# A list scheduler's table of operation times, latencies and landing times, refitted to recorded durations

## The chip, the cores and the metric

The kernel runs on one core of one Trainium2 chip. The metric is device time in microseconds. TensorE (PE) does matmuls and its weight loads (PEld in the profile), VectorE is DVE, ScalarE is ACT, GpSimd is POOL, and SyncE (SP) issues the DMAs.

## The reference, cut to what matters

A decoder trunk of two layers for 1024 tokens of width 1024. Layer 0 mixes tokens by a causal Conformer convolution, layer 1 by sliding-window attention (16 query heads, 4 key heads, window 128). After each mixer come a layer norm, an MLP with squared ReLU (width 4096), a second norm and a gated embedding of width 256:

```python
for i in range(DEPTH):
    if i < N_A_LAYERS:
        y = conformer_conv(x, conv_w_in[i], ...)          # x @ w_in, gate, depthwise conv, LN, SiLU, @ w_out
    else:
        kk, vv = shared_banded_kv(x, kv_w_k, kv_w_v, cos, sin)
        y = swa_sink_attention(x, attn_w_q[j], attn_sinks[j], attn_w_o[j], kk, vv, cos, sin)
    x = layer_norm(DEEPNORM_ALPHA * x + y, mix_ln_g[i], mix_ln_b[i])
    x = layer_norm(DEEPNORM_ALPHA * x + sq_relu_mlp(x, mlp_w_up[i], mlp_w_down[i]), mlp_ln_g[i], mlp_ln_b[i])
    x = x + (p[i] @ ple_w_proj[i]) * jax.nn.sigmoid(x @ ple_w_gate[i])
```

## The kernel before

**Arithmetic.** Every operand of a matmul is held as two parts: a high part (ScalarE copies it to the type fp32r) and a low part (VectorE subtracts the high part from the value); `split` (L719) makes both, and `mm3` (L723) spends three matmuls on a product, high by high, high by low and low by high. In the profile's names h and l at the end of a tile's name are these parts: wh and wl of a weight, xh and xl of x. Large products are cut by two-by-two schemes with seven products instead of eight, so sums of weight blocks and of token blocks (forms) are made on VectorE ahead of them; some forms are stored to DRAM (`gate_t`, `gate_low_t`, `hid`) and loaded again.

**Stages**, in the order of the program, with their time in the profile before: the convolution and its output product (`conv`, L883, `conv_seven` L940, `mix_out` L1333) up to about 250 us; the first MLP (`mlp` L1486, `down_seven` L1641), up to about 1015; the first gated embedding (`ple`, L1765), up to about 1080; attention (`attention`, L1915), up to about 1390, its output product and norm up to about 1430; the second MLP up to about 2010; the second embedding. Tokens go in tiles of 128 rows and columns in halves of 512, so that a matmul is mostly 128x512; a unit of weights is a tile of 128x1024 in raw (as loaded), wh and wl.

**Attention's values.** `values` (L2146) takes four heads of probabilities in z, transposes them on PE (ps<-ident,z), splits the result on ScalarE and VectorE into two tiles A, lets GpSimd mask both by affine_select into two more tiles A (`own_keys`, L2173), and multiplies all four by the values in v, z or bo.

**What sets the order.** No order is written out. The program is recorded first: `Recorder` keeps every operation with its inputs, its tiles and a priority, which is the place in the program plus an offset. `schedule` (L337) is a list scheduler: it always takes the engine that is free first, and on it the operation of the lowest priority that is ready by its own clock. Its clock has four parts: `cost` (L306) gives the length of an operation, `delay` in `schedule` the time from the end of one operation to the start of another that needs it, the block on SP the time at which a DMA lands, and `both` holds VectorE and GpSimd apart where it deems them to share a port. Tiles get slots from pools (SLOTS, L52: five slots for t, nine for A, six PSUM banks for ps), and a slot goes to the next tile in line when its last user has ended by that clock. Operations marked "either" (adds of the layer norm in `layer_norm`, L812ff, and of the embedding, L1801) go to VectorE or to GpSimd, whichever the clock has free first. `issue` (L478) then emits the operations in the order found, so all instructions carry its line, L488 (L499 after the change). On the chip each engine runs its instructions in this order and waits on semaphores, so the clock's numbers act through the order, the slots and the engine of the "either" adds, and through nothing else.

The functions that the diff touches, and what calls them:

Of the kernel before, what the change touches and what calls it, by code (L numbers as in the profile page):

```python
# [13 lines left out]
ALU = mybir.AluOpType  # L14
# [6 lines left out]
HT = 512  # L21
# [57 lines left out]
MIX_WORK = (2, 4), (0,)  # L79
UP_NEXT = 4, 6, 0, 2  # L80
DOWN_WORK = {0: [("w_q", range(4))], 1: [("w_q", range(4, 8))], 2: [("w_o", range(4))], 3: [("w_o", range(4, 8))]}, {}
Q_AHEAD = 2
PAIRS_AHEAD = (0,), (0, 2)
GRAIN = 64
# [131 lines left out]
class Recorder:  # L216
# [90 lines left out]
    def cost(self, o, outs, allv):  # L307
        e, n = o.eng, o.name
        f = outs[0].n if outs and isinstance(outs[0], View) else 1024
        if e == "tensor":  # L310
            if n == "transpose":
                return 113.5
            return max(109.0, f * 0.4427 + 5.5 * (f < HT))
        if e == "sync":
            return 380.0
        if e == "scalar":
            t = 60.0 + f * 0.85
            if n == "activation":
                t += sum(c for k, c in (("bias", 90.0), ("scale", 130.0), ("accum_out", 110.0)) if isinstance(o.kw.get(k), View))
            return t  # L320
        if e == "gpsimd":
            if n == "tensor_tensor":
                return 460.0 if o.kw["op"] == ALU.pow else 120.0 + 2.3 * f
            return 160.0 + 1.17 * f
        psum = any(v.buf.space == "PSUM" for v in allv)
        if n == "tensor_scalar" and not psum:
            return 100.0 + f * 0.69
        if n == "bn_stats":
            return 69.0 + 1.042 * allv[-1].n
        if n == "reduce_max":  # L330
            return 70.0 + allv[-1].n * 1.042
        if n == "reciprocal":
            return 60.0 + 6.3 * f
        t = 120.0 if isinstance(o.kw.get("scalar"), View) else 70.0
        return t + f * 1.042

    def schedule(self):  # L337
        import heapq
# [25 lines left out]
        dma = 0.0  # L364
        lanes = [0.0] * 8
        order = []
        lat = 200.0
        same = dict(vector=127.0, scalar=93.0, gpsimd=100.0)

        def delay(o, x):  # L370
            a, b = o.eng, x.eng
            if a in ("alloc", "sync") or b == "alloc":
                return 0.0
            if a == b:
                return same.get(a, 0.0)
            return 200.0 if a == "tensor" else 400.0 if b == "tensor" else 240.0

        def enable(o):
            if o.eng == "alloc":
# [44 lines left out]
        while True:  # L424
            best = None
            for e in engs:
                while rdy[e] and rdy[e][0][2].end:
                    heapq.heappop(rdy[e])
                while fut[e] and fut[e][0][3].end:
                    heapq.heappop(fut[e])  # L430
                if rdy[e]:
                    t = free[e]
                elif fut[e]:
                    t = max(free[e], fut[e][0][0])
                else:
                    continue
                if best is None or t < best[0]:
                    best = (t, e)
            if best is None:
                break  # L440
            t, e = best
            while fut[e] and fut[e][0][0] <= t:
                r, p, i, o = heapq.heappop(fut[e])
                if not o.end:
                    heapq.heappush(rdy[e], (p, i, o))
            p, i, o = heapq.heappop(rdy[e])
            if WAIT and fut[e] and e != "tensor":
                r, p2, i2, o2 = fut[e][0]
                if not o2.end and r <= t + WAIT and p2 < p - 300:
                    heapq.heappush(rdy[e], (p, i, o))  # L450
                    heapq.heappop(fut[e])
                    t, o = r, o2
            if o.eng == "either":
                o.eng = e
                o.dur = self.cost(o, o.outv, o.allv)
            d = o.dur
            if e == "scalar" and o.name == "activation":
                k = TABLE.get(o.args[2].name if len(o.args) > 2 else "", 0)
                if k and k != table:
                    table = k  # L460
                    d += 1283.0
            if both(o):
                d += max(0.0, held["gpsimd" if e == "vector" else "vector"] - 50.0 - t)
                held[e] = t + d
            free[e] = t + d
            if e == "sync":
                lane = max(t, lanes.pop(0))
                free[e] = lane + d
                dma = max(dma, lane + 1400.0) + max(v.transfer() for v in o.allv)
                lanes.append(max(dma, lane + 4000.0))  # L470
                finish(o, lanes[-1])
            else:
                finish(o, t + d)
# [47 lines left out]
class Emit:  # L521
# [964 lines left out]
    def mlp(self, i):  # L1486
# [90 lines left out]
        for n, cs in enumerate(DOWN):  # L1577
            self.down_seven(i, cs, n == 0, n == len(DOWN) - 1, list(range(NT)) if n == RES else [])
            nc.slack = WORK_SLACK
            for what, ks in DOWN_WORK[i].get(n, ()):  # L1580
                for k in ks:
# [748 lines left out]
```

## Time and profile before

| | us |
|---|---|
| three runs of the kernel | 2099.75, 2100.91, 2102.42 |
| their median | 2100.91 |
| the profiled execution | 2101.52 |
| its span (first to last instruction) | 2099.8 |
| PE busy, DVE busy, ACT busy, POOL busy | 2082.9, 1700.9, 1207.1, 295.1 |

A row of the timeline has the start, the length, the engine, the operation and its tiles (result <- sources, without slot numbers), and, in brackets, the idle time of the engine ahead of it with what ended that. A run of equal instructions stands in one row with its count (x4), its length from the first start to the last end. Matmuls overlap in their records.

### The profile page before, as it was taken

The numbers are of one execution on the slowest core, as the hardware profiler recorded it, in microseconds if no ns is written. First come the engines' busy times: TensorE is split into PE (matmuls) and PEld (weight loads), VectorE is DVE, ScalarE is ACT, GpSimd is POOL, SyncE is SP. The second block draws the span as 40 slices with busy tenths as digits, with TensorE's granted clock in tenths as the row PEclk, the third lists the DMA queues.
The fourth block names the chain that finished last, engine by engine and source line by source line (L and its number), as shares of the span: only waits on it lengthen the run. The fifth ranks groups of instructions, "written<-read, shape, count | busy, mean of one in ns | idle before, by whom it ended". The sixth has DMA issues, their size and how long they took to land.

```text
span 2099.8 us, 29286 instructions
## 1 busy us (share of the span) xinstructions
PE 2082.9 (99%) x9784; PEld 1729.3 (82%) x9784; DVE 1700.9 (81%) x2631; ACT 1207.1 (57%) x2224; POOL 295.1 (14%) x513
## 2 busy tenths in 40 slices
PE   9999999999999999999999999999999999999999
PEld 7888888888888888888888888877888888888877
DVE  8999789987876889987963587989787778888688
ACT  6777654766666644345742488656666563333374
POOL 0533114000000000002220265520000000000040
PEclk9999999999999999999999999999999999999999
DMA  6669864878776879875566877587878785575635
GB/s 226 192 202 296 294 197 143 298 265 273 269 270 216 307 257 319 279 262 215 171 211 192 319 227 238 188 298 249 269 259 275 254 285 200 181 247 171 233 126 191
DMA packets 239063, 502.01 MB, mean 239 GB/s; under 512 B 24128, under 2 KB 62784, under 8 KB 238912
## 3 DMA queue, kind: packets, MB, share of 16 engines
q1 hardware_dynamic: 238912, 500.14, 71.2%
q8 instruction: 77, 1.26, 0.2%
q14 instruction: 74, 0.61, 0.1%
HBM read 337.26 MB, written 160.17 MB: 237 GB/s over the span
## 4 chain that ended last, share of the span: by engine, by line
PE 88%; DVE 5%; DMA 3%; ACT 2%; issue 1%; POOL 1%; SPq 0%; DVEq 0%; ACTq 0%; POOLq 0%
PE ps L488 67%; PE tr L488 21%; DVE z L488 1%; DMA wh<-gate_t 1%; ACT z L488 1%; DVE g L488 1%; POOL sm L488 1%; DMA raw<-in_w_up_dram 1%; DVE wl L488 1%; DVE B L488 1%; DVE xl L488 0%; DVE t L488 0%; DVE v L488 0%; DVE sm L488 0%; DVE X L488 0%
## 5 line engine op out<-in xcount | busy, mean ns | idle before, releaser
L488 PE MATMUL ps<-xh,xl 128*128 128x512 f32 x618 | 240.5, 389 | 0.0
L488 PE MATMUL ps<-xl,xh 128*128 128x512 f32 x618 | 240.5, 389 | 0.0
L488 PE MATMUL ps<-xh 128*128 128x512 f32 x618 | 240.5, 389 | 0.0
L488 POOL TENSOR_SCALAR sm<-sm 128x1 f32<-128x1 f32 x72 | 26.8, 374 | 1362.9 <-DVE E L488 1200.1
L488 PE MATMUL ps<-xl,wh 128*128 128x512 f32 x536 | 210.3, 393 | 0.4 <-DVE xl L488 0.4
L488 PE MATMUL ps<-xh,wh 128*128 128x512 f32 x536 | 209.4, 393 | 0.8 <-DVE xl L488 0.5
L488 PE MATMUL ps<-xh,wl 128*128 128x512 f32 x536 | 210.0, 392 | 0.0
L488 ACT CAST wh<-raw 128x1024 fp32r<-128x1024 f32 (+2 forms) x130 | 115.5, 890 | 77.5 <-PE ps L488 47.9
L488 PE MATMUL ps<-wh,xh 128*128 128x512 f32 (+1 forms) x352 | 138.5, 395 | 3.2 <-DMA wh<-gate_t 1.2
L488 PE MATMUL ps<-wh,xl 128*128 128x512 f32 (+1 forms) x352 | 138.6, 394 | 0.1
L488 PE MATMUL ps<-wl,xh 128*128 128x512 f32 (+1 forms) x352 | 138.6, 394 | 0.0
L488 ACT CAST xh<-wh 128x1024 fp32r<-128x1024 f32 x76 | 79.7, 1049 | 99.7 <-PE ps L488 53.0
L488 PEld LDWEIGHTS ps<-xh 128*128 128x128 f32 x618 | 116.0, 188 | 24.2
L488 PEld LDWEIGHTS ps<-xh,xl 128*128 128x128 f32 x618 | 116.0, 188 | 24.1
L488 ACT CAST wh<-g 128x512 fp32r<-128x512 f32 x136 | 81.2, 618 | 94.9 <-PE ps L488 52.6
L488 PEld LDWEIGHTS ps<-xl,xh 128*128 128x128 f32 x618 | 116.1, 188 | 23.9
L488 DVE TENSOR_TENSOR wl<-raw,wh 128x1024 fp32r<-128x1024 f32 (+2 forms) x96 | 93.2, 972 | 37.0 <-ACT wh L488 35.8
L488 DVE TENSOR_TENSOR wl<-g,wh 128x512 fp32r<-128x512 f32 x136 | 90.9, 690 | 38.5 <-ACT wh L488 38.4
L488 PEld LDWEIGHTS ps<-xh,wh 128*128 128x128 f32 x536 | 100.9, 188 | 21.9 <-DVE xl L488 0.7
L488 PEld LDWEIGHTS ps<-xl,wh 128*128 128x128 f32 x536 | 101.0, 188 | 21.1 <-DVE xl L488 1.1
L488 PEld LDWEIGHTS ps<-xh,wl 128*128 128x128 f32 x536 | 100.9, 188 | 20.7
L488 ACT ACTIVATE t<-t 128x512 f32<-128x512 f32 x144 | 90.8, 632 | 34.9 <-DVE t L488 33.3
(406 smaller groups left out, 5644.6 us busy)
## 6 DMA issues: line engine op xcount, KB each, us to landing
wh<-hid SPq DMA_DIRECT2D x78, 512.0 KB, 4.6
raw<-in_w_up_dram SPq DMA_DIRECT2D x68, 512.0 KB, 4.3
wl<-in_w_down_dram SPq DMA_DIRECT2D x58, 512.0 KB, 5.3
hid<-zz SPq DMA_DIRECT2D x96, 256.0 KB, 4.8
hid<-t SPq DMA_DIRECT2D x64, 256.0 KB, 4.7
z<-in_w_dw_dram SPq DMA_DIRECT2D x56, 288.0 KB, 4.1
raw<-hid SPq DMA_DIRECT2D x30, 512.0 KB, 4.7
xh<-in_w_gate_dram SPq DMA_DIRECT2D x32, 256.0 KB, 5.6
```

The costliest lines, as they stand in the source:

```text
L488: getattr(getattr(nc, o.eng), o.name)(*a, **k)
```

## The change

Three constants are new, and `cost`, `delay` and the landing time take other numbers. The operations, their priorities, the pools and the rest of the scheduler are the same. Of the numbers: a scalar operation of 512 columns goes from 495 to 475 ns with a PSUM operand and to 522 without; a GpSimd add of 512 from 1298 to 1610, an affine_select of 512 from 759 to 623, a GpSimd operation of one column from 161 to 272, its power from 460 to 545; between engines, PE to others goes from 200 to 297 (358 to GpSimd), others to PE from 400 to between 360 and 403; a DMA lands 700 later where the transfers before it set its time.

```diff
+TO_PE = 300.0
+MARGIN = 100.0
+LANDING = 700.0
...
         if e == "tensor":
-            if n == "transpose":
-                return 113.5
-            return max(109.0, f * 0.4427 + 5.5 * (f < HT))
+            return 109.0 if n == "transpose" else max(109.0, (f + 32) / 2.4)
...
         if e == "scalar":
-            t = 60.0 + f * 0.85
+            t = 40.0 + 0.85 * f if psum else 95.0 + 0.833 * f
             if n == "activation":
-                t += sum(c for k, c in (("bias", 90.0), ("scale", 130.0), ("accum_out", 110.0)) if isinstance(o.kw.get(k), View))
+                t += sum(c for k, c in (("bias", 90.0), ("scale", 95.0), ("accum_out", 96.0)) if isinstance(o.kw.get(k), View))
...
         if e == "gpsimd":
             if n == "tensor_tensor":
-                return 460.0 if o.kw["op"] == ALU.pow else 120.0 + 2.3 * f
-            return 160.0 + 1.17 * f
+                return 545.0 if f == 1 else 100.0 + 2.95 * f
+            if n == "memset":
+                return 85.0 + 0.82 * f
+            if n == "affine_select":
+                return 60.0 + 1.1 * f
+            if n == "tensor_copy":
+                return 120.0 + f
+            return 272.0 if f <= 8 else 170.0 + 1.3 * f
+        if n == "tensor_copy" and not psum:
+            return 65.0 + 0.52 * f
...
-        t = 120.0 if isinstance(o.kw.get("scalar"), View) else 70.0
-        return t + f * 1.042
+        if n == "bn_aggr":
+            return 118.0
+        return 66.0 + f * 1.042
...
-        same = dict(vector=127.0, scalar=93.0, gpsimd=100.0)
+        same = dict(vector=130.0, scalar=137.0, gpsimd=100.0)
+        seen = dict(tensor=163.0, vector=95.0, scalar=103.0, gpsimd=60.0)
...
-            return 200.0 if a == "tensor" else 400.0 if b == "tensor" else 240.0
+            return seen[a] + (TO_PE if b == "tensor" else MARGIN + (95.0 if b == "gpsimd" else 34.0))
...
-                lanes.append(max(dma, lane + 4000.0))
+                lanes.append(max(dma + LANDING, lane + 4000.0))
```

What the new clock does to the order: PE has the same 9784 matmuls, of which 2902 stand at another place, by 2.1 places on average and 76 at most; the first difference is at 20.8 us of the profile before, and in 400 to 1000 and 1500 to 2000 us PE's order hardly differs. On DVE 2036 of 2597 operations move, on ACT 1099 of 2058, on POOL 364 of 511, and of SP's 1500 DMAs 793. Ten "either" adds go from DVE to POOL and eight from POOL to DVE. Slots are dealt out anew. Three places follow, each with the rows of the order, the kernel before first.

PE in the first embedding, around 1026 us. tr and ps5 (after: ps1) are results of gate products, wh4 with wl4 (after: wl2) the unit of `gate_t` whose load waits for a slot, and B3 and B6 tiles that PE transposes. The rows begin with the last matmuls that read the unit before it in that slot.

```order
L488 MATMUL tr1_1747_9862<-wh1_1654_9307,xh10_245_309 128x512
L488 MATMUL ps1_1744_9843<-ident_239_303,B3_1402_7196 128x128 x4
L488 MATMUL tr1_1747_9862<-wl0_1642_9221,xh10_245_309 128x512
L488 MATMUL ps2_1746_9857<-ident_239_303,B6_1404_7200 128x128 x4
L488 MATMUL tr1_1747_9862<-wh1_1654_9307,xl10_246_310 128x512
L488 MATMUL ps5_1749_9875<-wh3_1657_9347,xh11_708_2961 128x512
```

```order
L499 MATMUL ps4_1748_9867<-ident_239_303,B3_1399_7191 128x128 x4
L499 MATMUL tr0_1747_9860<-wh0_1655_9311,xl10_246_310 128x512
L499 MATMUL ps1_1760_9912<-wh1_1659_9352,xh11_710_2973 128x512
L499 MATMUL ps1_1760_9912<-wl0_1658_9348,xh11_710_2973 128x512
L499 MATMUL ps1_1760_9912<-wh1_1659_9352,xl11_726_3060 128x512
L499 MATMUL ps2_1753_9890<-ident_239_303,B6_1401_7194 128x128 x4
```

The two groups of four transposes stand one to six rows nearer to the matmul that waits for the load.

DVE in the second MLP, ahead of 1488 us. raw1 is a weight unit that a DMA brings, g are forms of it, t and z the tiles of hidden tokens; the last row is the one that frees the slot of t.

```order
L488 TENSOR_TENSOR g3_2658_14752<-raw1_2668_14813 128x512
L488 TENSOR_TENSOR t4_2655_14728<-t4_2655_14728,tr1_2618_14489 128x512
L488 TENSOR_TENSOR g0_2660_14765<-g3_2658_14752,raw0_2659_14759 128x512
L488 TENSOR_TENSOR wl1_2674_14861<-g3_2658_14752,wh3_2673_14858 128x512
L488 TENSOR_TENSOR g2_2662_14774<-raw0_2659_14759,raw1_2668_14813 128x512
L488 TENSOR_TENSOR zz0_2669_14833<-z2_2619_14493,bo0_2631_14558 128x512
L488 TENSOR_TENSOR wl1_2674_14861<-g0_2660_14765,wh3_2673_14858 128x512
L488 TENSOR_TENSOR zz0_2669_14833<-zz0_2669_14833,t2_2602_14392 128x512
L488 TENSOR_TENSOR z2_2619_14493<-t2_2602_14392,z2_2619_14493 128x512
```

```order
L499 TENSOR_TENSOR t2_2655_14731<-t2_2655_14731,ps0_2618_14482 128x512
L499 TENSOR_TENSOR g3_2658_14754<-raw1_2668_14814 128x512
L499 TENSOR_TENSOR g2_2662_14776<-raw0_2659_14760,raw1_2668_14814 128x512
L499 TENSOR_TENSOR g1_2660_14767<-g3_2658_14754,raw0_2659_14760 128x512
L499 TENSOR_TENSOR wl0_2674_14859<-g3_2658_14754,wh1_2673_14857 128x512
L499 TENSOR_TENSOR zz0_2669_14835<-z3_2619_14485,bo0_2631_14557 128x512
L499 TENSOR_TENSOR wl0_2674_14859<-g1_2660_14767,wh1_2673_14857 128x512
L499 TENSOR_TENSOR zz0_2669_14835<-zz0_2669_14835,t0_2603_14395 128x512
L499 TENSOR_TENSOR z3_2619_14485<-t0_2603_14395,z3_2619_14485 128x512
```

The add into t stands ahead of the operation that needs the loaded raw1, and no longer behind it.

PE in attention, around 1273 us. A4 (after: A2 and A4) with v are products of probabilities and values, ps3 (after: ps2) transposes of other probabilities, and tr<-wh,xh the next query product.

```order
L488 MATMUL ps0_2236_12551<-A4_2221_12468,v0_2198_12378 128x512
L488 MATMUL ps3_2214_12446<-ident_239_303,z0_2210_12426 128x128 x3
L488 MATMUL ps0_2236_12551<-A1_2225_12483,v0_2198_12378 128x512
L488 MATMUL ps5_2246_12604<-B0_1867_10506,X4_2131_12068 128x256
L488 MATMUL ps5_2246_12604<-E2_1873_10540,X4_2131_12068 128x256
L488 MATMUL tr0_2168_12237<-wh1_2127_12054,xh10_245_309 128x512
```

```order
L499 MATMUL ps3_2238_12570<-A2_2223_12483,v0_2202_12392 128x512
L499 MATMUL ps1_2240_12580<-B1_1874_10565,X5_2154_12179 128x256
L499 MATMUL ps1_2240_12580<-E2_1873_10551,X5_2154_12179 128x256
L499 MATMUL ps2_2218_12470<-ident_239_303,z3_2213_12439 128x128 x2
L499 MATMUL tr1_2166_12233<-wh0_2122_12037,xh10_245_309 128x512
L499 MATMUL tr1_2166_12233<-wl1_2123_12039,xh10_245_309 128x512
L499 MATMUL tr1_2166_12233<-wh0_2122_12037,xl10_246_310 128x512
L499 MATMUL tr1_2166_12233<-wh0_2122_12037,xh10_245_309 128x512
L499 MATMUL tr1_2166_12233<-wl1_2123_12039,xh10_245_309 128x512
L499 MATMUL tr1_2166_12233<-wh0_2122_12037,xl10_246_310 128x512
L499 MATMUL ps3_2238_12570<-A4_2226_12496,v0_2202_12392 128x512
```

Between the product's first and second matmul stood three transposes; now six matmuls of the query product stand there as well.

More of the change, by code (lines that the diff above doesn't have):

```diff
@@ L310, in cost @@
         if e == "tensor":
-            if n == "transpose":
-                return 113.5
-            return max(109.0, f * 0.4427 + 5.5 * (f < HT))
+            return 109.0 if n == "transpose" else max(109.0, (f + 32) / 2.4)
         if e == "sync":
             return 380.0
+        psum = any(v.buf.space == "PSUM" for v in allv)
         if e == "scalar":
-            t = 60.0 + f * 0.85
+            t = 40.0 + 0.85 * f if psum else 95.0 + 0.833 * f
             if n == "activation":
-                t += sum(c for k, c in (("bias", 90.0), ("scale", 130.0), ("accum_out", 110.0)) if isinstance(o.kw.get(k), View))
+                t += sum(c for k, c in (("bias", 90.0), ("scale", 95.0), ("accum_out", 96.0)) if isinstance(o.kw.get(k), View))
             return t
@@ L322, in cost @@
             if n == "tensor_tensor":
-                return 460.0 if o.kw["op"] == ALU.pow else 120.0 + 2.3 * f
-            return 160.0 + 1.17 * f
-        psum = any(v.buf.space == "PSUM" for v in allv)
+                return 545.0 if f == 1 else 100.0 + 2.95 * f
[8 more added lines that the diff above has]
+            return 65.0 + 0.52 * f
         if n == "tensor_scalar" and not psum:
```

## The prediction

> **What bounds the kernel now.** I read the page's engine shares first, then the busy time of each engine by stretch, then what TensorE (PE) waited for, then the instructions around the longest of those waits.
>
> ```profile
> PE 2082.9 (99%) x9784; PEld 1729.3 (82%) x9784; DVE 1700.9 (81%) x2631; ACT 1207.1 (57%) x2224; POOL 295.1 (14%) x513
> ```
>
> PE is busy for 2082.9 of 2099.8 us, so 16.9 us hold no matmul record, the start and the end of the program among them. No order of the same work can win more than that and the little that each pause hides. It hides some because a 128x512 matmul is recorded with 0.39 us, while its successors start 0.23 us apart, as here:
>
> ```profile
> 1025.53 0.39 PE L488 MATMUL ps<-wl,xh 128*128 128x512 f32 x1
> 1025.76 0.40 PE L488 MATMUL ps<-wh,xl 128*128 128x512 f32 x1
> 1026.48 0.50 PE L488 MATMUL ps<-wh,xh 128*128 128x512 f32 x1 [0.33 <-DMA wh<-gate_t]
> 1026.82 0.40 PE L488 MATMUL ps<-wl,xh 128*128 128x512 f32 x1
> ```
>
> From 1025.76 to 1026.82 are two starts, worth 2 x 0.23 = 0.46 us, and it took 1.06: 0.60 us are lost where the idle column shows 0.33. I therefore price each pause from start to start, at 0.23 us a matmul.
>
> ```profile
> 250.00:270.00 20.00, 18.01 (x96) 14.36 (x95) 18.17 (x46) 14.73 (x34) 12.18 (x20) 1.00 0.98 346
> 270.00:1015.00 745.00, 744.81 (x3356) 616.96 (x3354) 621.12 (x909) 418.08 (x658) 51.16 (x66) 1.00 0.73 248
> 1190.00:1290.00 100.00, 99.10 (x544) 81.88 (x543) 84.98 (x182) 84.62 (x287) 67.22 (x171) 1.00 0.71 229
> 1390.00:1432.00 42.00, 39.80 (x181) 31.42 (x180) 41.65 (x69) 25.97 (x45) 6.88 (x7) 1.00 0.88 317
> 1490.00:2010.00 520.00, 520.00 (x2303) 430.40 (x2302) 407.52 (x569) 264.17 (x399) 12.02 (x20) 1.00 0.69 231
> 2040.00:2075.00 35.00, 34.06 (x153) 27.96 (x152) 34.04 (x55) 15.90 (x27) 1.58 (x1) 1.00 0.60 202
> ```
>
> The columns are window, length, busy PE, PEld, DVE, ACT, POOL, clock, DMA share and GB/s. In 270 to 1015 and 1490 to 2010 PE never stops (744.81 of 745, 520 of 520): 60% of the span, where a better order has nothing to win and a worse one something to lose. The granted clock is 1.00 throughout, so no order gains by it. PE pauses in the short stretches. In 1390 to 1432 VectorE (DVE) is busy for 41.65 of 42 us and is the bound itself; in 2040 to 2075 it is nearly so (34.04 of 35).
>
> ```profile
> PE ps L488 <- DVE t L488: 2.4, 2, 1.5
> PE ps L488 <- DMA wh<-gate_t: 1.2, 2, 0.9
> PE ps L488 <- DVE xl L488: 1.2, 4, 0.5
> PE tr L488 <- DMA wh<-gate_t: 0.9, 1, 0.9
> PE ps L488 <- DMA B<-scr: 0.5, 1, 0.5
> PE ps L488 <- POOL A L488: 0.2, 1, 0.2
> ```
>
> These rows (total, times, longest) show single late events of 0.2 to 1.5 us, not a queue of one cause. So the change is a sum over places.
>
> **The change part by part.** No instruction is added or removed; 2902 of PE's 9784 matmuls change place, by 2.1 places on average, and 2036 of DVE's 2597 operations. Engines run in order, so a new table of costs acts only through this order, through the slots that tiles get, and through which engine does an add that may run on DVE or GpSimd (POOL). For each pause I ask how much PE work the new order puts between what is waited for and the waiting matmul.
>
> *The load at 1026.* The row above waits for a gate weight whose DMA starts when its slot comes free. In the new order two groups of four transposes stand behind that release instead of ahead of it. A transpose starts 0.08 to 0.15 us after the one before it; these rows give both:
>
> ```profile
> 1076.29 1.05 PE L488 MATMUL ps<-ident,B 128*128 128x128 f32 x6 [0.25 <-DVE xl L488]
> 1077.18 0.49 PE L488 MATMUL tr<-ident,B 128*128 128x128 f32 x3
> 1077.43 0.48 PE L488 MATMUL ps<-wh,xh 128*128 128x512 f32 x1
> ```
>
> (0.89 / 6 and 0.25 / 3.) Eight are 0.64 to 1.2 us, either of them over the 0.60 that is lost: **-0.6**. If the slot comes free later, nothing is won (0).
>
> *The transposes at 1076* in the same rows wait for DVE; the new order has about 0.9 us more work ahead of three of them. I take the **-0.4** that the row and its 0.25 idle bear (bounds 0 and -0.65). The load at 1059 (the 0.9 of the gate rows) gets 0.9 us more cover too, but its low part is now issued ahead of it, and I count it at 0 (bounds +0.4, one more issue of 0.4 us as below, and -0.9).
>
> *The stall at 1488*, the largest of the second half:
>
> ```profile
> 1486.87 0.39 PE L488 MATMUL tr<-xl,wh 128*128 128x512 f32 x1
> 1488.42 0.73 PE L488 MATMUL ps<-A,wh 128*128 128x512 f32 x2 [1.16 <-ACT t L488]
> 1488.99 0.40 PE L488 MATMUL ps<-A,wl 128*128 128x512 f32 x1
> 1486.42 0.68 DVE L488 TENSOR_TENSOR zz<-zz,t 128x512 f32<-128x512 f32 x1
> 1487.03 0.68 DVE L488 TENSOR_TENSOR z<-t,z 128x512 f32<-128x512 f32 x1
> 1487.79 0.58 ACT L488 COPY t<-ps 128x512 f32<-128x512 f32 x1 [1.93 <-issue]
> ```
>
> Three starts took 2.12 instead of 0.69: 1.43 us lost. PE waits for ScalarE's copy, this for a slot of t that z<-t,z frees, and DVE comes to it in an unbroken row of operations 0.60 us apart, behind a weight's DMA. In the new order one add (t<-t,tr in the rows of the change) goes ahead of the operation that waits for the DMA: six instead of seven stand between that one and z<-t,z, 0.60 us sooner. Two more matmuls (0.46) stand ahead of the waiting one: **-1.05** (0 if the DMA sets it, -1.43 at most).
>
> *Attention, 1200 to 1340.*
>
> ```profile
> 1272.65 0.49 PE L488 MATMUL ps<-ident,z 128*128 128x128 f32 x3
> 1273.41 0.50 PE L488 MATMUL ps<-A,v 128*128 128x512 f32 x1 [0.28 <-DVE A L488]
> 1273.86 0.36 PE L488 MATMUL ps<-B,X 128*128 128x256 f32 x1
> 1281.83 0.71 PE L488 MATMUL ps<-A,bo 128*128 128x512 f32 x2
> 1282.78 0.50 PE L488 MATMUL ps<-A,bo 128*128 128x512 f32 x1 [0.24 <-POOL A L488]
> 1283.24 0.39 PE L488 MATMUL ps<-raw,X 128*128 128x256 f32 x1
> ```
>
> The first loses 1.21 - 3 x 0.11 - 0.23 = 0.65 (0.11 is the middle of the two transpose paces), the second 1.41 - 3 x 0.23 = 0.72. Ahead of the first the new order moves six 128x512 matmuls (1.38 us), ahead of the second some 2.7 us of work; both go: **-1.4**. Four smaller pauses that the list of waits doesn't show I leave at 0. Elsewhere in attention the new order takes work away from between producer and consumer: at four or five places PE's lead shrinks to under a microsecond. I price four new pauses at 0.3, the middle of the idle rows above: **+1.2** (0 if none binds; +2.9 if each is as long as the 0.72).
>
> *The layer norm at 250 to 270 and the wait for B<-scr.* Two groups of transposes move behind 1.1 us of other work, and one statistic behind the cast that PE needs. Against them the norm's own chain starts no earlier, and this stretch lacks 2.0 us of PE. I take **-0.5** (between -2.5 and +2.0).
>
> *1390 to 1432: 0.* One add goes to POOL, a DVE operation of 0.69 less. But:
>
> ```profile
> 1396.98 1.74 POOL L488 TENSOR_TENSOR B<-z,g 128x512 f32<-128x512 f32 x1 [0.30 <-DVE sm L488]
> 1396.89 0.68 DVE L488 TENSOR_TENSOR X<-X,X 128x512 fp32r<-128x512 f32 x1
> 1397.49 1.78 DVE L488 TENSOR_TENSOR z<-z,g 128x512 f32<-128x512 f32 x1
> ```
>
> DVE's multiply, due at 1397.49, ends at 1399.27, 0.55 us after POOL's add ends (1398.72); its neighbour took 0.68. A POOL add thus costs DVE up to 1.78 - 0.68 = 1.1 us, more than the 0.6 that it takes off it: between -0.6 and +0.5. [...]
>
> *2040 to 2075: 0.*
>
> ```profile
> 2068.47 0.38 SPq L488 DMA_DIRECT2D wh<-gate_t  x1
> 2073.96 0.47 PE L488 MATMUL tr<-wh,xh 128*128 128x512 f32 x1 [0.94 <-DMA wh<-gate_t]
> ```
>
> The load follows DVE's unbroken row, and PE's work between slot and use shrinks by 1.8 us while the load is asked for sooner; I can't tell which prevails (bounds -1.2 and +1.8).
>
> **Sum:** -0.6 - 0.4 - 1.05 - 1.4 - 0.5 + 1.2 = -2.75. The profiled execution took 2101.52 us (span 2099.8 and 1.7 around it), 0.6 above the median of 2100.91; so 2098.8 on its own basis, and on the median's 2100.91 - 2.75 = **2098.2**.
>
> **The rivals.**
>
> *A, the next wait takes the place of each.* Where DVE is busy without a break, a pause that goes at one matmul comes back at a later one, since DVE ends no sooner. For it speak 1390 to 1432 and 2040 to 2075; against it, that behind 1488 and in 270 to 1015 PE runs free for hundreds of microseconds. The -1.05 and -0.6 stay, the rest is repaid: 2100.91 - 1.65 + 1.2 = 2100.5.
>
> *B, the table is right nearly everywhere.* Then most of the 16.9 us goes, save the start and end (about 6): 2100.91 - 11 = 2090. For it: some new numbers stand nearer to the rows than the old. A POOL add of 512 was planned with 1298 ns, now with 1610:
>
> ```profile
> L488 POOL TENSOR_TENSOR E<-z,g 128x512 f32<-128x512 f32 x16 | 26.0, 1635 | 5.8 <-DVE z L488 4.2 <-issue 1.0 <-DVE sm L488 0.6
> L488 POOL TENSOR_SCALAR_AFFINE_SELECT A<-A 128x512 fp32r<-128x512 f32 x56 | 38.4, 690 | 17.1 <-ACT A L488 10.3 <-DVE A L488 4.2 <-PE tr L488 0.8
> ```
>
> Against it: the norm's chain and the DVE-bound stretches are no matter of order.
>
> *C, slower: POOL's masks in attention come late.* The affine_select was planned with 759 ns and 400 to PE, 1159 in all, and is now planned with 623 + 360 = 983, while the rows above say 690 on average. So PE's matmul is put up to 176 ns nearer to each of 56 masks. If all run out of lead that costs 56 x 0.176 = 9.9 us, and with the attention's -1.4 lost: 2100.91 - 1.35 + 9.9 = 2109.5. It is slower by 0.2% (4.2) from 32 late masks on. Against it: 690 is still 290 short of 983, and only one of 56 masks is in the list of waits now (0.2).
>
> That the change does nothing can't be: 30% of the matmuls move.
>
> **How the numbers follow.** A measurement of this kernel tells about 0.2%, 4.2 us, from no change. My forecast has .46 (.18 of it below 2096.7, where new pauses don't bind, .28 within), A .17 (within), B .20 (faster), C .17 (slower; with it every other way in which thinner leads cost more than they bring). Faster .38, same .45, slower .17. The likeliest case's own range is 2094 to 2102: its places don't all err to one side, and about half of what their bounds add up to is allowed for. The range for 8 in 10 reaches to 2089 for B and to 2107 for C with 43 masks of 56 late.
>
> **What would show it.** In the new profile: no wait for gate_t near 1026, under 0.5 us lost at 1488, the waits for DVE A and POOL A gone and new ones of about 0.3 us for A or z in 1200 to 1340; 1390 to 1432 as long as before. Rival A shows as the same total of PE waits at other rows, B as a list of PE's waits that sums to under 4 us, C as many waits for POOL A. I am wrong if 270 to 1015 or 1490 to 2010, where PE never stopped, hold waits, or if a stall of over 2 us stands where none was.

## The result, and the profile after

The changed kernel takes 2109.2 us (median of 6 runs, 2106.03 to 2110.62) against 2101.28 for the kernel before (6 runs, 2099.24 to 2104.62): a ratio of 1.0034, 95% interval 1.0021 to 1.0047. On a second chip it was 1.0028 (1.0019 to 1.0037). The forecast was 2098.2 with a range to 2107; the time went the other way, and out of the range. The profiled execution took 2109.34 us with a span of 2107.6, 7.8 more than before.

The page of the changed kernel, and some of PE's longest waits (total, times, longest):

```profile
PE 2084.9 (99%) x9784; PEld 1731.2 (82%) x9784; DVE 1699.1 (81%) x2629; ACT 1208.2 (57%) x2224; POOL 298.9 (14%) x515
```

```profile
PE ps L499 <- POOL B L499: 2.9, 3, 1.6
PE tr L499 <- issue: 2.1, 1, 2.1
PE ps L499 <- DMA wh<-gate_t: 2.0, 2, 1.5
PE tr L499 <- POOL A L499: 1.5, 1, 1.5
```

PE is busy 2.0 us longer with the same matmuls, which is already odd, and without work for 22.7 us instead of 16.9. The waits for GpSimd are new in this size: 2.9 us for B and 1.5 for A, where the list of before had 1.2 and 0.2:

```profile
PE ps L488 <- POOL B L488: 1.2, 2, 1.0
```

The 2.1 us under issue, for which the list names nobody, are PE's longest single wait. They stand in the second embedding, and VectorE's rows show what they wait for, an add that reads the PSUM bank that PE's matmul writes:

```profile
2076.99 0.69 DVE L499 TENSOR_TENSOR zz<-zz,tr 128x512 f32<-128x512 f32 x1
...
2077.78 0.47 PE L499 MATMUL tr<-wh,xh 128*128 128x512 f32 x1 [2.10 <-issue]
```

The add ends at 2077.68, 0.10 us ahead of PE's start. The second trace of the changed kernel has the same pause, of 2.13 us, as close behind the same add; in the kernel before PE did not wait at this matmul.

Four of the windows that the prediction shows for before, now in the changed kernel (window, length, busy PE, PEld, DVE, ACT, POOL, clock, DMA share, GB/s):

```profile
250.00:270.00 20.00, 17.57 (x88) 14.32 (x87) 19.35 (x47) 14.16 (x33) 10.98 (x20) 0.91 0.96 335
270.00:1015.00 745.00, 743.42 (x3343) 615.35 (x3342) 616.29 (x905) 414.79 (x654) 50.97 (x63) 1.00 0.73 249
1390.00:1432.00 42.00, 39.13 (x180) 31.87 (x179) 40.27 (x61) 25.24 (x42) 13.78 (x11) 0.96 0.85 286
1490.00:2010.00 520.00, 519.56 (x2291) 429.74 (x2291) 406.52 (x566) 261.61 (x393) 5.88 (x12) 1.00 0.69 233
```

Two things are to be seen. The long stretches of the MLPs are as full as before, but for one pause of 1.5 us after 270. And the granted clock, 1.00 in all four of them before, is 0.91 and 0.96 in the two stretches with a layer norm: this is why PE is busy for longer with the same work.

To see where the 7.8 us lie, the next table compares stretches that hold the same matmuls. Time lost is the time from the end of one matmul to the end of the next, less 0.2267 us for a 128x512 matmul, 0.120 for 128x256 and 0.109 for a transpose, summed over a stretch (limits in us of the profile before). The changed kernel has two traces, from two chips; the other columns are explained with the experiments.

| stretch of before | before | changed | changed, again | nudge | add longer | changed, old add |
|---|---|---|---|---|---|---|
| 0 to 240 | 7.54 | 7.73 | 8.99 | 8.56 | 12.29 | 7.85 |
| 240 to 276, norm of the first mixer | 3.28 | 4.95 | 5.07 | 3.50 | 6.74 | 3.14 |
| 276 to 310 | 0.11 | 1.83 | 1.87 | 0.16 | 1.65 | 2.09 |
| 310 to 1015, first MLP | 1.29 | 1.32 | 1.02 | 0.91 | 1.88 | 0.75 |
| 1015 to 1080, first embedding | 2.75 | 3.51 | 2.16 | 3.00 | 6.07 | 5.02 |
| 1080 to 1350, attention | 6.06 | 8.18 | 7.90 | 8.33 | 5.75 | 7.86 |
| 1350 to 1440, norm of the second mixer | 4.41 | 5.56 | 6.83 | 10.13 | 7.81 | 4.32 |
| 1440 to 2010, second MLP | 2.26 | 1.78 | 1.08 | 0.92 | 0.45 | 1.17 |
| 2010 to 2100 | 3.43 | 4.12 | 4.64 | 2.79 | 5.63 | 1.83 |
| sum | 31.1 | 39.0 | 39.6 | 38.3 | 48.3 | 34.0 |

So the 7.8 us are the norm at 240 to 310 (+3.4), attention (+2.1), the norm at 1350 to 1440 (+1.2), the two embeddings (+0.8 and +0.7), less 0.5 in the second MLP.

**The pause behind 276.** PE waited for A at 286.95, and GpSimd's multiply that makes it took 4.98 us. PE, GpSimd and VectorE of the changed kernel:

```profile
286.95 0.55 PE L499 MATMUL tr<-ident,A 128*128 128x128 f32 x3 [1.50 <-POOL A L499]
...
281.91 4.98 POOL L499 TENSOR_SCALAR A<-A,sm 128x512 f32<-128x512 f32 x1 [3.31 <-issue]
...
281.67 0.68 DVE L499 TENSOR_TENSOR E<-E,bo 128x512 f32<-128x512 f32 x1
282.27 0.54 DVE L499 TENSOR_SCALAR X<-X,sm 128x512 f32<-128x512 f32 x1
282.72 3.09 DVE L499 TENSOR_TENSOR E<-E,bo 128x512 f32<-128x512 f32 x5
285.74 0.68 DVE L499 TENSOR_TENSOR B<-B,bo 128x512 f32<-128x512 f32 x1
286.67 0.51 DVE L499 CAST xh<-t 128x512 fp32r<-128x512 f32 x1 [0.25 <-ACT t L499]
```

VectorE runs without a gap from 281.67 to 286.42, and the multiply ends at 286.89, 0.47 us behind the start of that gap; in the second trace it took 4.98 us as well and ended as far behind. In the kernel before another such multiply took 0.77 us and this very one 1.33, ahead of the row of VectorE adds:

```profile
271.58 0.77 POOL L488 TENSOR_SCALAR A<-A,sm 128x512 f32<-128x512 f32 x1 [2.03 <-DVE sm L488]
275.01 1.33 POOL L488 TENSOR_SCALAR A<-A,sm 128x512 f32<-128x512 f32 x1 [0.36 <-issue]
```

**The norm at 1400.** GpSimd's power took 1.48 us, in the same interval as a wide VectorE subtraction, where it took 0.55 before; behind it PE waited three times for B, and then ran at half pace:

```profile
1402.94 1.48 POOL L499 TENSOR_TENSOR sm<-sm,mhalf 128x1 f32<-128x1 f32 x1
...
1402.80 1.22 DVE L499 TENSOR_TENSOR wl<-raw,wh 128x1024 fp32r<-128x1024 f32 x1
...
1407.02 0.66 PE L499 MATMUL ps<-ident,B 128*128 128x128 f32 x4 [0.23 <-POOL B L499]
1409.30 0.66 PE L499 MATMUL ps<-ident,B 128*128 128x128 f32 x4 [1.62 <-POOL B L499]
1410.97 1.97 PE L499 MATMUL ps<-ident,B 128*128 128x128 f32 x8 [1.02 <-POOL B L499]
1412.72 0.80 PE L499 MATMUL ps<-xh,wh 128*128 128x512 f32 x1
1413.32 0.63 PE L499 MATMUL ps<-xl,wh 128*128 128x512 f32 x1
```

Eight transposes take 1.75 us from the first start to the next matmul, 0.22 each, and 128x512 matmuls start 0.43 to 0.60 apart, where 0.11 and 0.23 are usual.

### The profile page after: what moved, and what is told of

It is laid out like the page before. It is cut to its first block, busy times and chain, and to the rows that moved or that the text cites. A ratio compares the mean times of both kernels' runs of the same rounds, so it can differ in the third digit from the quotient of the medians.

```text
span 2107.6 us, 29311 instructions
## 1 busy us (share of the span) xinstructions
PE 2084.9 (99%) x9784; PEld 1731.2 (82%) x9784; DVE 1699.1 (81%) x2629; ACT 1208.2 (57%) x2224; POOL 298.9 (14%) x515
## 5 line engine op out<-in xcount | busy, mean ns | idle before, releaser
L499 PE MATMUL ps<-xh 128*128 128x512 f32 x636 | 247.4, 389 | 0.0
L499 PE MATMUL ps<-xl,xh 128*128 128x512 f32 x636 | 247.4, 389 | 0.0
L499 PE MATMUL ps<-xh,xl 128*128 128x512 f32 x636 | 247.4, 389 | 0.0
L499 PE MATMUL ps<-xh,wh 128*128 128x512 f32 x504 | 197.0, 393 | 2.1 <-ACT xh L499 2.0
L499 PE MATMUL ps<-xl,wh 128*128 128x512 f32 x504 | 197.6, 392 | 0.0
L499 PE MATMUL ps<-xh,wl 128*128 128x512 f32 x504 | 197.1, 391 | 0.0
L499 PEld LDWEIGHTS ps<-xh,wh 128*128 128x128 f32 x504 | 94.8, 188 | 22.5 <-ACT xh L499 2.4
L499 DVE TENSOR_TENSOR t<-t,ps 128x512 f32<-128x512 f32 (+1 forms) x111 | 76.0, 685 | 45.3 <-PE ps L499 32.5
L499 DVE TENSOR_TENSOR xl<-wh,xh 128x1024 fp32r<-128x1024 f32 x76 | 92.8, 1221 | 22.2 <-ACT xh L499 19.4
L499 PEld LDWEIGHTS ps<-xh,wl 128*128 128x128 f32 x504 | 94.9, 188 | 19.3
```

What stands on the lines that cost most here:

```text
L499: getattr(getattr(nc, o.eng), o.name)(*a, **k)
```

## The experiments

Two groups. The first (e5 to e8) edits the changed kernel at single places, with its order otherwise kept, to see whether the mechanisms above cost what they seem to. The second gives the scheduler one part of the new table at a time, or a number that refits nothing, to see which part of the change does it. "Before" in each is the kernel before, run on the same chip between the others.

**e5: one GpSimd multiply issued to VectorE.** The edit, in `issue`, after the order is made:

```diff
+        for o in order:
+            if o.num == 3183:
+                o.eng = "vector"
```

> The changed kernel, in which the one multiply A<-A,sm that took 4.98 us on GpSimd at 281.91 us is issued to VectorE instead, at the same place in the order; nothing else moves. [...] Rival (the chain is late anyway): PE waits there for the rest of the norm's chain, under 0.5 us comes back, and the time stays at 2108.7 to 2109.2.

Measured: 2107.8 us, ratio 1.0023 (1.0013 to 1.0033). In its trace:

```profile
282.11 0.53 DVE L505 TENSOR_SCALAR A<-A,sm 128x512 f32<-128x512 f32 x1
...
284.86 0.49 PE L505 MATMUL tr<-ident,A 128*128 128x128 f32 x3
285.10 0.47 PE L505 MATMUL ps<-wh,xh 128*128 128x512 f32 x1
```

The multiply takes 0.53 us, PE doesn't wait, and the stretch 276 to 310 loses 0.12 us instead of 1.83. Locally the whole pause goes, 1.71 us, where the rival lets under 0.5 come back; the median fell by 1.4, which the spread of the runs would hardly show by itself.

This trace shows something else as well. Up to 281 us its order is that of the changed kernel, and PE's two long pauses in the norm are the same (1.02 and 1.41 us idle), but its clock stays at 1.00. In the changed kernel's trace the two stretches at half clock are 3.413 us long each (263.86 to 267.27, 1410.74 to 1414.15), and their starts are 336 such lengths apart; a third begins at 2107.06, 540 lengths behind the first. So I cut each trace into windows of this length, placed by its own stretches. The changed kernel first, then e5:

```profile
260.45:263.86 3.41, 1.25 (x10) 0.79 (x8) 3.34 (x8) 3.41 (x8) 3.10 (x6) 1.00 1.04 338
263.86:267.27 3.41, 3.14 (x11) 2.66 (x12) 3.41 (x10) 1.61 (x4) 3.23 (x5) 0.50 0.89 296
```

```profile
259.89:263.30 3.41, 2.39 (x18) 1.78 (x17) 3.34 (x9) 2.41 (x6) 3.17 (x7) 1.00 1.04 374
263.30:266.72 3.42, 2.01 (x16) 1.57 (x14) 3.42 (x9) 2.42 (x6) 3.25 (x5) 1.00 0.98 283
```

In the changed kernel most of both pauses falls into one window, in which PE is busy for 1.25 us, and the next window runs at 0.50. In e5 they are split between two windows. The stretch 240 to 276 loses 3.5 us in e5, against 4.95 in the changed kernel and 3.28 before: nearly all that the changed kernel loses there is the half clock. In these two traces it comes or not with the place at which the windows fall (260.45 and 259.89), which differs between two executions whose order is the same up to there.

**e6: PE kept busy in its pauses.**

```diff
+FILL = {3278: 14, 13937: 14, 13964: 9}
...
+                for _ in range(FILL.get(o.num, 0)):
+                    nc.tensor.transpose((a[0] if a else k["out"])[:, 0:P], ident, ident)
```

> The changed kernel with 37 idle transposes put into PE's three longest pauses in the two layer norms: 14 of the identity ahead of the matmul that waited 1.97 us at 264.13, 14 and 9 ahead of the transposes that waited 1.84 and 1.39 us at 1409.30 and 1410.97. They write the bank that the waiting matmul overwrites. Theory (the granted clock falls because PE stood idle): PE is busy in these pauses, the clock stays at 1.00 in both stretches (0.50 and 0.68 before), and the matmuls behind them run at full pace: 1.3 + 1.4 us come back, 2106.5 in all, although work was added. Rival (the clock falls for another reason): the clock is 0.50 there as before and the time is 2109.2 or up to 1 us more.

The clock by windows, changed kernel first, then e6:

```profile
262.00:264.00 2.00, 0.72 (x5) 0.49 (x5) 2.00 (x6) 2.00 (x5) 1.83 (x5) 0.96 0.99 302
264.00:266.00 2.00, 1.87 (x6) 1.58 (x7) 2.00 (x6) 0.23 (x1) 1.92 (x3) 0.50 0.84 248
```

```profile
262.00:264.00 2.00, 2.00 (x20) 1.84 (x18) 2.00 (x7) 2.00 (x5) 1.83 (x5) 1.00 0.80 236
264.00:266.00 2.00, 2.00 (x13) 1.72 (x13) 2.00 (x4) 0.99 (x4) 1.92 (x3) 1.00 1.02 307
```

PE works in the pause, and the clock stays at 1.00. From the matmul that had waited to the same later one it is 4.75 us in the changed kernel (264.13 to 268.88) and 3.29 in e6 (263.98 to 267.27):

```profile
264.13 0.79 PE L499 MATMUL ps<-wh,xh 128*128 128x512 f32 x1 [1.41 <-DVE xh L499]
...
268.88 0.48 PE L499 MATMUL ps<-wl,xh 128*128 128x512 f32 x1
```

```profile
263.98 0.50 PE L504 MATMUL ps<-wh,xh 128*128 128x512 f32 x1
...
267.27 0.48 PE L504 MATMUL ps<-wl,xh 128*128 128x512 f32 x1
```

So the half clock costs 1.46 us there. Around 1410 it is less, 0.6 at first: PE then waits 0.48 for VectorE, which the slow transposes had covered. From 1414 on only 0.2 are left, behind a wait for a load. Together that is 1.6 us, and the trace has a span of 2105.9, 1.7 less than the changed kernel's. As to the whole, the median was 2109.26 (2106.65 to 2113.35), ratio 1.0031 (1.002 to 1.0043). The fill did its work in the other executions too, with a mean clock of 0.999 to 1.000 where the changed kernel has 0.997 to 0.999, but the 1.6 us do not appear in the median; the interval, 2.4 us to each side, neither shows nor excludes them.

**e7: a wide VectorE subtraction moved out of the norm's way.**

```diff
+        order.remove(n[14011])
+        order.insert(order.index(n[13962]) + 1, n[14011])
```

> The changed kernel, in which one VectorE operation, the low part wl<-raw,wh of 128x1024 at 1402.80 us, is issued behind the norm's last add at 1410.32 instead; its first reader comes at 1426.7. Theory (it held up GpSimd's power, 1.48 us instead of 0.55, and so the whole chain of the norm): the power takes 0.55 to 0.6, the chain is 0.9 us earlier, PE's pauses at 1407 to 1411 sum to 2.8 instead of 3.7 us, and the time is 2108.3, or 2106.9 if the shorter pauses keep the clock at 1.00. Rival (VectorE is the bound there, so that the 1.2 us come back a few operations later): pauses move behind 1411 and the time is 2109.2, within 0.4.

Measured: 2111.36 us, ratio 1.0042 (1.0029 to 1.0054), slower than both expected. GpSimd and PE:

```profile
1401.10 0.55 POOL L505 TENSOR_TENSOR sm<-sm,mhalf 128x1 f32<-128x1 f32 x1
...
1406.69 0.66 PE L505 MATMUL ps<-ident,B 128*128 128x128 f32 x4 [1.59 <-POOL B L505]
...
1411.25 0.80 PE L505 MATMUL ps<-xh,wh 128*128 128x512 f32 x1 [1.62 <-DVE xl L505]
1417.10 0.80 PE L505 MATMUL tr<-xh,wl 128*128 128x512 f32 x1 [1.64 <-DMA wl<-form]
```

The power takes 0.55, so the wide subtraction was what held it up. But the 1.2 us stand in VectorE's row again, ahead of the subtraction that PE waits for at 1411.25, and a load comes late at 1417. The subtraction was the last reader of a slot of raw, and SP issued the next load into raw at 1410.06, just behind it (it ended at 1409.99); the wl<-form of the wait stands behind that load in SP's queue, at 1411.93 (1409.90 in the changed kernel). With these pauses the granted clock is 0.50 for 10.2 us (1410.54 to 1420.78) instead of 3.4. The rival was right in its kind, and short by the DMA queue and the clock.

**e8: the three edits together.**

> The three edits of the other kernels of this call together. Theory (three separate places): their gains add: 2109.2 - 1.7 - 2.7 - 0.9 = 2103.9. Rival (what one place wins, the next one loses, since VectorE has no time left): 2107 or more.

Measured: 2114.31 us, ratio 1.0048 (1.0036 to 1.0061). The rival holds: the gains don't add. In the trace the first two are there (3.2 us by 310), but around 1410 it loses 5.6, since the third edit's late load is longer here (PE idle for 3.57 us ahead of a matmul at 1417.96).

**The parts of the table.** Each of the next is the kernel before with a part of the change, or the changed kernel with a part taken back; the diffs name the numbers.

```diff
 e1   lanes.append(max(dma + 700.0, lane + 4000.0))
 e2   same, seen, TO_PE, MARGIN and delay() as in the change
 e3   cost() as in the change
 e4   scalar: t = 62.0 + f * 0.85   (before: 60.0)
 e4b  same = dict(vector=129.0, ...)   (before: 127.0)
 e9   cost(): the gpsimd lines alone
 e10  cost(): all but the gpsimd lines
 e11  the changed kernel with the gpsimd lines of before
 e12  gpsimd: one-column operations 272, power 545
 e13  gpsimd: the other new lines (adds 100 + 2.95 f, affine_select 60 + 1.1 f, ...)
 e14  gpsimd: adds 100 + 2.95 f, nothing else
 e15  the changed kernel with adds 120 + 2.3 f
 e16  as e13 with adds 120 + 2.3 f
```

> The changed kernel itself once more, so that the parts beside it are read against it on one chip. Both theories: 2107 to 2111, 0.3% above the kernel before.

> The kernel before with the landing time alone changed (700 ns more where the transfers before set it). Theory L (the loss comes from particular numbers, those of the operations' lengths and latencies around the layer norms, where VectorE and GpSimd collide): the norms keep their order, waits on gate weights shrink by up to 0.6 each, and the time is within 1.5 us of before's. Theory D (the kernel before is a lucky draw: any table that deals the order anew loses about as much, whatever the numbers): 4 to 9 us slower than before.

> The kernel before with the latencies between engines alone changed (the table of same-engine times, the times seen, TO_PE and MARGIN). Theory L: these numbers set how far PE runs ahead of its producers; attention loses 1 to 2 us as in the changed kernel and the norms up to 2: 2103 to 2105. Theory D: 4 to 9 us slower than before, at places that differ from those of the changed kernel.

> The kernel before with the lengths of operations alone changed. Theory L: the GpSimd lengths decide where the norm's operations stand; most of the loss comes with them, the pauses at 287 (1.7 us) and around 1410 (3.7 us) among it: 2106 to 2109. Theory D: 4 to 9 us slower as well, but with pauses at other places, so that the three parts together lose more than twice the 7 us of the whole change.

Measured: the changed kernel 2108.63 (1.0028); e1 2104.82 (1.0013, 1.0005 to 1.0022), e2 2105.87 (1.0011, 1.0002 to 1.002), e3 2115.83 (1.006, 1.0047 to 1.0072). The lengths alone cost twice what the whole change costs, and landing and latencies a little each. Theory L named the lengths rightly, but not that they would cost more by themselves; theory D's 4 us and more did not come for e1 and e2, and e1's 2.7 us (1.0013) lie above theory L's 1.5, though the interval reaches below it. D's other claim held: the three parts together lose 0.84%, three times the 0.28% of the whole change.

> The kernel before with one number nudged: a scalar operation is planned 2 ns longer (60 to 62), which refits nothing but moves 1640 matmuls and 2004 VectorE operations. Theory D (the kernel before is a lucky draw among orders of this scheduler, any new deal loses): 2 to 8 us slower than before, at places like those of the changed kernel. Theory L (particular numbers of the table do it): within 1.5 us of before.

> The kernel before with VectorE's time between its own operations nudged by 2 ns (127 to 129): 288 matmuls and 818 VectorE operations move. Theory D: slower as well, in proportion to the places that it reaches, 1 to 4 us. Theory L: within 1 us of before.

> The kernel before with GpSimd's lengths alone changed. Theory L: the loss of the lengths (13.6 us when they alone were changed) is theirs, by the places of the norm's adds and masks: 2110 to 2116. Theory D: like any other new deal, 2103 to 2108.

> The kernel before with the lengths of PE, ScalarE and VectorE alone changed. Theory L (GpSimd's lengths carry the loss): within 3 us of before. Theory D: like any other new deal, 2103 to 2108; and the loss with GpSimd's lengths and this one need not sum to 13.6.

Measured: e4 2107.11 (1.0018, 1.0009 to 1.0027), e4b 2104.23 (1.0006, 0.9997 to 1.0015), e9 2116.54 (1.0063, 1.0051 to 1.0076), e10 2108.76 (1.0028, 1.0018 to 1.0038). Both theories are half right. A nudge that refits nothing costs 4 us when it moves 1640 matmuls: most of it at 1350 to 1440 and in attention (the column in the table, of an execution 1.5 us above that kernel's median). The one that moves 288 is not clear of nothing. e10 lost 5.6 us, more than either theory gave it. And GpSimd's lengths cost far more than a new deal does.

> The changed kernel with GpSimd's lengths of before put back, all other new numbers kept. Theory L (GpSimd's lengths carry what goes beyond a new deal): 2103 to 2106, better than the changed kernel by 3 to 6 us. Theory D (the sum of a deal is chance, whichever numbers make it): no better than the other deals, 2106 to 2110.

> The kernel before with the lengths of GpSimd's one-column operations alone changed (161 to 272, the power 460 to 545). Theory S (the norm's chain of small operations is planned as long as it lasts when VectorE holds it up, and is put in other places): most of the 13 us of GpSimd's lengths, 2110 or more. Theory W (the adds and masks of 512 columns do it): a plain new deal, 2103 to 2108.

> The kernel before with the lengths of GpSimd's wide operations alone changed (adds of 512 from 1298 to 1610, masks from 759 to 623, scalings of 128 from 310 to 336, memsets and copies). Theory W: 2110 or more. Theory S: a plain new deal, 2103 to 2108.

Measured: e11 2107.1 (1.0019, 1.001 to 1.0028), e12 2104.98 (1.0005, 0.9996 to 1.0014), e13 2124.81 (1.0103, 1.0089 to 1.0118). It is the wide operations. Taking GpSimd's lengths back leaves the price of a deal like the nudge's, and no gain over before, in the range of theory D and not of L.

> The kernel before with one length changed: a GpSimd add of 512 columns is planned with 1610 ns instead of 1298 (256 columns: 855 instead of 709). Theory W-add (the profile's undisturbed adds take 1292 to 1297, its mean of 1.6 us includes the time that VectorE holds them up; a table with the mean counts the hold twice, since the scheduler adds it by itself): most of the 22 us of the wide lengths, 2112 or more. Theory W-mask (the masks, planned shorter than they last, do it): a plain new deal, 2103 to 2108.

> The changed kernel with the length of GpSimd's adds alone put back to before's (1298 for 512 columns). Theory W-add: faster than the changed kernel by 3 us or more, 2103 to 2106. Rival (chance: the same number that costs 22 us in one deal does nothing in another): 2106 to 2111.

> The kernel before with GpSimd's other wide lengths changed, its adds not (masks of 512 from 759 to 623, scalings of 128 from 310 to 336, memsets and copies). Theory W-add: a plain new deal, 2102 to 2107. Theory W-mask: 2112 or more.

Measured: e14 2123.33 (1.0104, 1.0087 to 1.0121), e15 2106.12 (1.0017, 1.0008 to 1.0025), e16 2102.05 (1.0003, 0.9994 to 1.0012). One number, the add's 1610 for 1298, makes the whole loss of e13 (21.3 of 21.9 us); the masks make nothing. In the changed kernel the same number is worth about 3 us (1.0028 and 1.0034 against 1.0017), but the intervals overlap, and e15's 2106.12 lies on the border between the two ranges that were expected, so that chance is not excluded there. All tables together, by the matmuls that stand at another place than before:

| kernel | matmuls moved | ratio | add planned |
|---|---|---|---|
| e4b nudge | 288 | 1.0006 | 1298 |
| e16 | 1034 | 1.0003 | 1298 |
| e12 | 1191 | 1.0005 | 1298 |
| e4 nudge | 1640 | 1.0018 | 1298 |
| e2 latencies | 1797 | 1.0011 | 1298 |
| e10 | 1939 | 1.0028 | 1298 |
| e1 landing | 2307 | 1.0013 | 1298 |
| e11 | 2758 | 1.0019 | 1298 |
| e15 | 3088 | 1.0017 | 1298 |
| e14 | 1822 | 1.0104 | 1610 |
| e13 | 2414 | 1.0103 | 1610 |
| e3 | 2464 | 1.0060 | 1610 |
| e9 | 2582 | 1.0063 | 1610 |
| changed | 2902 | 1.0034, 1.0028 | 1610 |

Every table with the long add is at 1.0028 or above, every other at 1.0028 or below, and no table was faster than the kernel before. The number of moved matmuls does not set the loss by itself: e16 and e12 move over 1000, and are not clear of no change. Nor does the number of adds that GpSimd gets: of 512 columns it has 45 in e14, 45 in e1 and e4, and 42 before. In e14 the loss is spread: 4.8 us up to 240, 5.0 around the first norm (clock 0.94 in 230 to 290, where it was 1.00), 3.3 in the first embedding, 3.4 around the second norm. Its longest waits are for VectorE's subtractions:

```profile
PE ps L488 <- DVE xl L488: 5.9, 6, 2.8
```

Why 1610 is the worse number though the mean is 1.6 us is seen in the kernel before, GpSimd's adds by their names (total, mean ns):

```profile
L488 POOL TENSOR_TENSOR B<-v,g 128x512 f32<-128x512 f32 x2 | 2.6, 1292 | 3.4 <-issue 2.7 <-PE ps L488 0.7
L488 POOL TENSOR_TENSOR B<-B,bo 128x512 f32<-128x512 f32 x1 | 1.3, 1297 | 2.0 <-PE ps L488 2.0
```

E<-z,g takes 1635 on average, over 16 adds. Of all 42 adds of 512 columns in that trace 15 take 1273 to 1302 ns and 27 take 1582 to 2214, with none between. When one of the 27 starts, VectorE is at an operation whose tiles are all outside PSUM (z<-z,g for most of them); when one of the 15 starts, VectorE is idle or reads a PSUM tile (ps or tr). The mean of E<-z,g is that of 13 long ones and 3 short ones. So the old 1298 is the add's own length, and what is above it is time held up. The scheduler adds holds itself (`both`, `held`), so with 1610 it counts them twice, and holds VectorE back for each add by as much again in its own clock. That the double count is how the order becomes worse is argued from the code; that the number does it is shown by e14 to e16.

## Why the prediction was wrong

By its own steps, in microseconds of time lost against before:

- *The load at 1026, -0.6:* right in the first trace, where no wait of 0.1 or more is left. In the second, 0.30 us of idle stand there (at 1031.18), nearly as before.
- *The load at 1059, 0 (bounds +0.4 and -0.9):* out of its bounds on either side. In the first trace the load is asked for at 1057.54 and lands at 1064.56, 7.0 us later, where it was 5.0 before, and PE loses 1.76 instead of 1.10. In the second it lands after 5.5, and PE does not wait for it. I had bounded it by an issue on SP and not by the landing itself, which differs between executions of one order. And a new pause stands ahead of it in both traces, at 1059.08 and 1060.98 (0.97 and 1.20 lost): there PE starts 0.1 us behind a VectorE add that reads its bank, as at 2077.78.
- *The transposes at 1076, -0.4:* they are idle for 0.21 us instead of 0.25 in the first trace (at 1081.77), and not at all in the second: -0.2 and -0.6.
- *The stall at 1488, -1.05:* right in kind, -0.72:

```profile
1494.82 0.39 PE L499 MATMUL ps<-xh,wh 128*128 128x512 f32 x1
1495.65 0.73 PE L499 MATMUL ps<-A,wh 128*128 128x512 f32 x2 [0.44 <-ACT t L499]
1496.22 0.39 PE L499 MATMUL ps<-A,wl 128*128 128x512 f32 x1
```

  1.40 us for three starts, 0.71 lost instead of 1.43. In the second trace PE does not wait there.
- *Attention, -1.4 and +1.2:* it came to +2.1 (6.06 to 8.18). The two waits that I named did shrink, and other ones of 0.3 to 0.9 came, more and longer than four at 0.3; the longest:

```profile
1272.18 0.73 PE L499 MATMUL ps<-A,bo 128*128 128x512 f32 x2 [0.63 <-DVE A L499]
```

- *The norm at 250 to 270, -0.5:* +1.7, and +1.7 more behind 276, of which the prediction had nothing. The first is the half clock, as e5 shows: with the same order there and the clock at 1.00 it is +0.2. The prediction read "The granted clock is 1.00 throughout, so no order gains by it", and had no term for an order that loses by it. As to the second, it asked only about the pauses that the profile of before showed; the multiply that collides there was ahead of its row of adds then, and no wait pointed at it.
- *1390 to 1432, 0:* +1.2 and +2.4 in the two traces.
- *2040 to 2075, 0 (bounds -1.2, +1.8):* +0.7 and +1.2 behind 2010, inside, but by luck. The load that was bounded costs less (0.39 us of idle and none, instead of 0.94), and the 2.1 us for VectorE's add at 2077.78 are new. They are the "stall of over 2 us" that the prediction had named as a sign of being wrong; the other sign, a wait in 270 to 1015, came as well, at 286.95.

**The step that failed is the price of new pauses: "I price four new pauses at 0.3", for attention alone.** The new pauses came in both norms and both embeddings as well, behind VectorE or GpSimd: 1.5 us at 286.95, 2.1 at 2077.78, and 2.9 in three waits for B around 1409, where before had 1.2. By the nudge a new order alone can cost 4 us (1640 matmuls moved), with nothing in the numbers to earn it back, and the places of before that I priced singly add up to no more than that, 3.95. The second failure is in rival B, which took the add's 1610 for a better number because it is "nearer to the rows". It is the mean of a length and of collisions, and cost 21 us alone and, as far as the overlapping intervals tell, about 3 here.

Rival C, the slower one, had the right side by a wrong mechanism, which is luck: the masks in attention aren't what PE waits for (the 1.5 us for A are the norm's multiply), and e16 with the new mask length alone is at 1.0003. The price of a collision, 1.1 us for VectorE by the rows at 1397, was too small: GpSimd's multiply lost 4.2 in one (4.98 against 0.77).

What stays open: whether the 1.6 us of e6's trace are in its whole time; by which steps the add's length spoils the order in e14 (its losses lie in five stretches); what makes the new pauses in attention, which no experiment took apart; by what GpSimd and VectorE hold each other up, since the runs show the times alone, and a shared port is the scheduler's assumption; and whether the kernel before is the fastest by chance, or because its priorities and slots were chosen with the old table.

## What to carry to other kernels

A table of operation times for a scheduler should hold the undisturbed length (here 1292 to 1297 ns), not the recorded mean (1.6 us), where the scheduler models the disturbance itself. A refit is judged against nudges that refit nothing: here one nudge cost 0.18% and another, of fewer moves, 0.06%, which is not clear of nothing, so that a new table can start 4 us behind the order that it replaces. And a forecast of a new order must price what no wait of the old profile shows, above all short operations of GpSimd that now stand beside a long row of VectorE's (4.98 us here for a multiply that took 1.33 before).

## What the runs showed of the hardware that was not expected

- GpSimd's multiply A<-A,sm of 128x512 took 4.98 us in the changed kernel, beside an unbroken row of eight VectorE operations (281.67 to 286.42), and ended 0.47 us behind the start of the first gap. VectorE's X<-X,sm of 0.54 us (282.27) stood in that row, and the multiply did not end with it either.
- In the kernel before, whether a GpSimd add of 512 columns was held up went by what VectorE did as it started: 27 of 27 took 1582 ns or more beside an operation on tiles outside PSUM, 15 of 15 took 1302 or less otherwise.
- The granted clock fell to 0.50 in windows of 3.413 us, one at 263.86 and one at 1410.74 in the changed kernel, three in a row in e7 (1410.54 to 1420.78). The same two pauses brought it about where they fell into one window (PE busy for 1.25 of 3.41 us) and not where they were split between two (2.39 and 2.01, e5), nor where PE was given idle transposes in the second of them (e6, clock 1.00 in 262 to 266). No threshold can be read from these traces: in e2 a window with 1.91 us of busy PE (263.43 to 266.84) was followed by half clock, in e6 one with 1.59 (2074.34 to 2077.75) was not. Other executions of the kernel before have a mean clock of 0.998 too.
- One and the same DMA of 512 KB landed 7.0 us after its issue in one execution of the changed kernel and 5.5 in another.
